# A fixed TensorE order for a state-space stage, and other slabs and banks for the last attentions

## The chip, the cores and the metric

The kernel runs on one core of one Trainium2 chip. The metric is the device time of one launch in microseconds (us); a kernel's time is the median of its runs. Engines are TensorE (PE), VectorE (DVE), ScalarE (ACT), GpSimd (POOL) and SyncE (SP, whose queue issues most DMA transfers).

## What is computed

512 tokens of width 1024 in f32 pass four layers, each with an RMS norm ahead of it and a residual sum behind. The first two are an even layer (sliding-window attention beside a state-space mixer) and an odd one (top-k attention); the others are forgetful (fox) attention and dilated attention, each with a memory attention beside it and a convolutional FFN behind it. What the change touches of the reference:

```
def s5_mixer(u, ...):                       # G=32 groups of 16, P=64 states
    dt = exp(log_dt);  mag = exp(a_re * dt);  ang = a_im * dt
    ab = mag * (cos(ang) + i sin(ang));  bb = ((ab - 1) / a) * b
    bu = einsum('blgh,gph->blgp', ug, bb)
    x  = associative_scan(x[t] = ab * x[t-1] + bu[t])
    y  = einsum('blgp,ghp->blgh', x_re, c_re) - einsum(x_im, c_im) + d_skip * ug
    h  = gelu(y) @ glu_w + glu_b
    return h[..., :W] * sigmoid(h[..., W:])

def even_layer(hn, ...):
    q, k, v, gate_a, u, gate_b = split_cols(hn @ w_in, ...)
    att = swa_sink_attention(rms_norm(q), rms_norm(k), v, sinks, rel_bias) * silu(gate_a)
    ssm = s5_mixer(u, ...) * silu(gate_b)
    return concatenate([att, ssm]) @ w_out

# layers 3 and 4
    mix = fox_attention(q, k, v, log_f)        # or dilated_attention(q, k, v)
    h = h + concatenate([mix, memory_attention(qm, rmsnorm(mem), w_mem_kv)]) @ w_out
    h = h + conv_ffn(rmsnorm(h), ...)
```

## The kernel before

**Products and weights.** Every large product is three PE products of split operands (`mm3`, lines 221 to 223: high by high, low by high, high by low). A weight slab of 256 columns comes by `slab()` (line 196): two pieces, each a raw DMA of 512 KB into one of two raw buffers, a copy on ACT (line 216, the high part `wh`) and a subtraction on DVE or POOL (line 217, the low part `wl`). Slabs live in a ring of two buffers (`wp`), to which a phase may add a third.

**Order.** A scheduler arranges the instructions of each engine by when they can run. Where an order is wanted, code is emitted under `issue_after`; the class `Chain` uses it to line up PE's instructions one by one, and `Steps` puts pieces of work off by so many units. Before the change the attentions use `Chain` and the state-space stage does not.

**State-space stage** (lines 617 to 870). After the `u` products (`u2`), the 32 groups are handled in four quarters. `core_a(qu)` (line 634) makes the matrices of a quarter: `zb` on DVE (lines 650 to 652: two products and a sum, twice), `cp` on POOL (667 to 669), transposes of `zb` on PE (681) that ACT evacuates to `bt`, the product with `cbd` (687), `k0` (697), the turned input `uq` (706) and the product `bu` (715). `core_b(qu)` (line 719) runs the scan in DVE (lines 728 to 745, result `zz`), then the products `yp` on PE (755 on) and a gelu on ACT and DVE. Every second quarter `y` is transposed into `yh` and `yl`. The program's order is a(0), then a(qu+1), b(qu); the query products (eight units of a slab quarter, each with a head norm and a transpose) and the gate products (eight units) stand behind in the program and are moved forward by the scheduler as they fit. Behind the gates `gbr`, a bias row, opens the GLU.

**Attentions 3 and 4** (`attn34`, line 1306). Projections stream 13 slabs, then the units of the attention follow (scores, softmax on ACT, transposes of the probabilities `pt`, values `o`), and each block ends in `finish` (line 906): the output product with four slabs of `w_out`, the residual sum and the next norm, whose scaled block `xn` is transposed by `to_x` (line 272) in two halves, each into a PSUM bank that ACT (`xh`) and DVE (`xl`, line 282) evacuate. All four `w_out` slabs are asked for behind the last projection.

Of the kernel before, what the change touches and what calls it, by code (L numbers as in the profile page):

```python
# [8 lines left out]
F32 = mybir.dt.float32  # L9
# [88 lines left out]
def _build(tc, nc, ctx, t, out, dbg, upto):  # L98
# [97 lines left out]
    def slab(src, r0, kc, pieces, wpool=None):  # L196
# [8 lines left out]
        for k0 in range(0, kc, per):  # L205
            k1 = min(kc, k0 + per)
# [8 lines left out]
            with urgent() if evq[1] else nullcontext():  # L215
                A.activation(hi[:, k0:k1], raw, AF.Copy)  # L216
                eng.tensor_tensor(lo[:, k0:k1], raw, hi[:, k0:k1].bitcast(F32), op=OP.subtract)  # L217
        return hi, lo
# [29 lines left out]
    def norm_scale(hb, gb, xn):  # L248
# [4 lines left out]
        V.tensor_scalar(ss[:, 2:3], ss[:, 0:1], 1.0 / D, EPS, op0=OP.mult, op1=OP.add)  # L253
# [208 lines left out]
    normed = []  # L462

    def norm_half(half):
        for tb in (2 * half, 2 * half + 1):
            normed.append(norm_block1(xin[tb], gb, x1, tb, n0))
# [34 lines left out]
    for i in range(3):  # L501
        PE.transpose(prmps[:, i * 16:(i + 1) * 16], prm[:, i], ident[:16, :16])
# [115 lines left out]
    for cs_ in range(2):  # L618
        w = slab(w_in1, 0, 8, [(1280 + cs_ * 256, 256)])
        for i in range(4):  # L620
            ps = acc()
            tm(ps[:, :256], w, xk(x1, i * 128, i * 128 + 128))
            evac(u2[:, cs_ * 16:(cs_ + 1) * 16, i, :], ps[:, :256].rearrange("p (g x) -> p g x", x=16))
    dump("u2", u2)
# [9 lines left out]
    def core_a(qu):  # L634
# [58 lines left out]
        k0 = sp_.tile([128, 8, 8, 16], F32, tag="k0", name="k0", bufs=2)  # L693
        for th in range(2):
            tp = tps()
            for i in range(4):
                PE.matmul(tp[:, i * 128:(i + 1) * 128], shm[:, th * 4 + i], c7, start=True, stop=True)
            evac(k0[:, :, th * 4:(th + 1) * 4, :].rearrange("p g t o -> p t g o"),
                 tp.rearrange("p (t g o) -> p t g o", t=4, g=8))
# [3 lines left out]
        for g in range(8):  # L703
            for s2 in range(2):
                rs_ = slice(s2 * 64, s2 * 64 + 64)
                PE.matmul(tp[rs_, g * 64:(g + 1) * 64], u2[:, (g % 2) * 16 + g0 + g // 2].rearrange("p i x -> p (i x)"),
                          ident.rearrange("p (c s) -> p s c", s=2)[:, s2], start=True, stop=True)
        A.activation(uq.rearrange("p g c -> p (g c)"), tp, AF.Copy)

        bu = sps()  # L710
        buv = bu.rearrange("p (r g c) -> p r g c", r=2, g=4)
        for i in range(2):
            for g in range(4):
                for q in range(2):
                    PE.matmul(buv[q * 64:(q + 1) * 64, i, g], bt[:, i, g, q * 64:(q + 1) * 64], uq[:, 2 * g + q],
                              start=True, stop=True)
        cst_[qu] = (gs, cp, k0, uq, buv)

    def core_b(qu):
# [10 lines left out]
        zz = sp_.tile([128, 2, 4, 64], F32, tag="zz", name="zz")  # L730
# [6 lines left out]
        for i in range(2):  # L737
# [8 lines left out]
                               op1=OP.subtract)  # L746

        yp = pst("yp")
        ypv = yp.rearrange("p (t g o) -> p g t o", t=8, g=4)
        for g in range(4):  # L750
            for i in range(3):
                for q in range(2):
                    qs = slice(q * 64, q * 64 + 64)
                    if i < 2:
                        PE.matmul(ypv[qs, g], xs[qs, i, g], cp[qs, i, g],
                                  start=i == 0, stop=False)
                    else:
                        PE.matmul(ypv[qs, g], uq[:, 2 * g + q], k0[:, 2 * g + q],
# [952 lines left out]
```

## Time and profile before

| | us |
|---|---|
| three runs, median | 1884.34 (1881.91 to 1887.64) |
| profiled execution | 1881.42 |
| its span | 1879.6 |
| PE busy | 1781.7 (95%) |
| DVE, ACT, POOL busy | 1037.2, 734.8, 150.7 |
| chain that ended last | PE 78%, DVE 10%, DMA 4%, ACT 4%, issue 3% |

The span is what the profiler recorded of one execution; the execution's own time lies 1.8 us above it. The page divides the span into 40 equal slices of 47 us and gives the busy tenths of each engine and the granted PE clock of each, in tenths of full speed. The timeline rows give the idle time of an engine ahead of a group in square brackets, and what ended it. Since PE is busy 95% of the span, what matters is where its waits lie and which clock it was granted.

### The profile page before, as it was taken

The page shows a single profiled execution, that of the slowest core. Times are in us where ns is not written, and L with a number is a line of the kernel's source. Part 1 is how long each engine was busy: PE and PEld are TensorE (multiplying, and loading weights), DVE is VectorE, ACT ScalarE, POOL GpSimd, SP SyncE. Part 2 cuts the span into 40 slices and gives each one's busy share as a digit, 9 for nine tenths or more (in the row PEclk, how much of TensorE's full clock was granted, in tenths as well). Part 3 has the DMA queues.
Part 4 walks back from the last instruction along what each step waited for, and adds up shares of the span by engine and source line. Part 5 has one row for each costly group of instructions (what it writes and reads, how often), then busy time and mean ns, then how long its engine had stood idle before and what let it go on. Part 6 is the DMA issues. An engine that isn't in the chain of part 4 may idle for free.

```text
span 1879.6 us, 27744 instructions
## 1 busy us (share of the span) xinstructions
PE 1781.7 (95%) x11106; PEld 1511.3 (80%) x11108; DVE 1037.2 (55%) x2110; ACT 734.8 (39%) x1460; POOL 150.7 (8%) x159
## 2 busy tenths in 40 slices
PE   6889899999999998989999999999989999999998
PEld 5777689878688886778888888889957888888886
DVE  6865574279855525655655562266276555554522
ACT  5333353353434334543443342233265444333421
POOL 2432101222120000000000000000000000000000
PEclk9899999999999999999999999999999999999999
DMA  5403222312513332003333323333220133332321
GB/s 151 130 13 112 90 90 59 94 57 68 166 42 99 112 112 90 1 1 100 98 105 93 90 68 117 107 124 99 82 90 1 37 113 90 100 102 74 106 90 67
DMA packets 187896, 161.72 MB, mean 86 GB/s; under 512 B 14568, under 2 KB 170320, under 8 KB 187768
## 3 DMA queue, kind: packets, MB, share of 16 engines
q1 hardware_dynamic: 181168, 144.30, 24.8%
q0 software_dynamic: 2784, 9.00, 1.6%
q10 hardware_dynamic: 3816, 6.66, 1.1%
q8 instruction: 87, 1.43, 0.3%
q14 instruction: 41, 0.34, 0.1%
HBM read 157.88 MB, written 4.74 MB: 87 GB/s over the span
## 4 chain that ended last, share of the span: by engine, by line
PE 78%; DVE 10%; DMA 4%; ACT 4%; issue 3%; POOL 1%; SPq 0%; DVEq 0%; ACTq 0%; POOLq 0%
PE acc L221 19%; PE acc L222 19%; PE acc L223 19%; PE misc L351 6%; PE o L351 2%; DVE wl L217 2%; PE tps L351 2%; PE spp L351 1%; ACT wh L216 1%; PE misc L221 1%; PE misc L222 1%; PE misc L223 1%; PE o L1232 1%; ACT p L1475 1%; DMA raw<-in_ev_w_in_dram 1%
## 5 line engine op out<-in xcount | busy, mean ns | idle before, releaser
L217 DVE TENSOR_TENSOR wl<-raw,wh 128x1024 fp32r<-128x1024 f32 (+3 forms) x242 | 296.3, 1234 | 392.3 <-ACT wh L216 392.0
L216 ACT ACTIVATE wh<-raw 128x1024 fp32r<-128x1024 f32 (+2 forms) x262 | 270.2, 1044 | 488.9 <-PE acc L222 208.1
L222 PE MATMUL acc<-xl,wh 128*128 128x512 f32 (+2 forms) x1064 | 402.3, 379 | 0.5 <-DVE xl L282 0.5
L221 PE MATMUL acc<-xh,wh 128*128 128x512 f32 (+2 forms) x1064 | 402.2, 380 | 0.5 <-ACT xh L281 0.5
L223 PE MATMUL acc<-xh,wl 128*128 128x512 f32 (+2 forms) x1064 | 400.7, 377 | 0.0
L223 PEld LDWEIGHTS acc<-xh,wl 128*128 128x128 f32 (+1 forms) x1064 | 201.4, 189 | 39.2
L221 PEld LDWEIGHTS acc<-xh,wh 128*128 128x128 f32 (+1 forms) x1064 | 200.7, 189 | 40.0 <-ACT xh L281 1.0
L222 PEld LDWEIGHTS acc<-xl,wh 128*128 128x128 f32 (+1 forms) x1064 | 201.5, 189 | 39.0 <-DVE xl L282 0.8
L221 PE MATMUL acc<-wh,xh 128*128 128x256 f32 (+1 forms) x704 | 204.6, 291 | 2.4 <-ACT xh L281 1.9
L223 PE MATMUL acc<-wh,xl 128*128 128x256 f32 (+1 forms) x704 | 200.9, 286 | 0.6 <-DVE xl L282 0.6
L222 PE MATMUL acc<-wl,xh 128*128 128x256 f32 (+1 forms) x704 | 200.5, 285 | 0.7 <-DVE wl L217 0.7
L221 PEld LDWEIGHTS acc<-wh,xh 128*128 128x128 f32 x704 | 134.8, 192 | 10.4 <-issue 5.8
L223 PE MATMUL acc<-wh,gl 128*128 128x512 f32 x352 | 139.2, 395 | 0.0
L221 PE MATMUL acc<-wh,gh 128*128 128x512 f32 x352 | 138.5, 394 | 0.0
L222 PE MATMUL acc<-wl,gh 128*128 128x512 f32 x352 | 138.5, 393 | 0.0
L222 PEld LDWEIGHTS acc<-wl,xh 128*128 128x128 f32 x704 | 134.9, 192 | 1.6 <-DVE wl L217 1.0
L223 PEld LDWEIGHTS acc<-wh,xl 128*128 128x128 f32 x704 | 135.0, 192 | 1.2 <-DVE xl L282 1.0
L256 POOL TENSOR_TENSOR rs<-ss,mhalf 128x1 f32<-128x1 f32 x32 | 18.2, 569 | 1413.6 <-DVE ss L254 1341.0
L351 PE MATMUL misc<-wh,ah 128*128 128x256 f32 x280 | 83.9, 300 | 3.8 <-DVE xl L282 3.8
L351 PE MATMUL misc<-wh,al 128*128 128x256 f32 x280 | 81.2, 290 | 2.0 <-DVE al L1514 2.0
L351 PE MATMUL misc<-wl,ah 128*128 128x256 f32 x280 | 81.0, 289 | 0.0
L222 PEld LDWEIGHTS acc<-wl,gh 128*128 128x128 f32 x352 | 66.2, 188 | 15.6
(1380 smaller groups left out, 3057.2 us busy)
## 6 DMA issues: line engine op xcount, KB each, us to landing
raw<-in_w_up_dram SPq DMA_DIRECT2D x176, 256.0 KB, 3.2
raw<-in_w_down_dram SPq DMA_DIRECT2D x44, 512.0 KB, 3.6
raw<-in_od_w_in_dram SPq DMA_DIRECT2D x24, 512.0 KB, 3.5
raw<-in_w_in_dil_dram SPq DMA_DIRECT2D x20, 512.0 KB, 3.5
raw<-in_ev_w_in_dram SPq DMA_DIRECT2D x18, 512.0 KB, 3.7
raw<-in_w_out_dram SPq DMA_DIRECT2D x16, 512.0 KB, 3.9
raw<-in_w_in_fox_dram SPq DMA_DIRECT2D x14, 512.0 KB, 4.6
raw<-in_ev_w_out_dram SPq DMA_DIRECT2D x8, 512.0 KB, 3.4
```

The source lines that it names most:

```text
L216: A.activation(hi[:, k0:k1], raw, AF.Copy)
L217: eng.tensor_tensor(lo[:, k0:k1], raw, hi[:, k0:k1].bitcast(F32), op=OP.subtract)
L221: pe.matmul(ps, lh, rh, start=first, stop=False)
L222: pe.matmul(ps, lh, rl, start=False, stop=False)
L223: pe.matmul(ps, ll, rh, start=False, stop=last)
L256: G.tensor_tensor(r, ss[:, 3:4], mhalf[:, :1], op=OP.pow)
L351: self.last = op(*a, **k).ins
L1232: PE.matmul(pov[:, hd % 4], vt[:, kb, kv * 128:(kv + 1) * 128], pt_[:, kb * 128:(kb + 1) * 128], start=kb == 0, stop=kb == qb)
L1475: A.activation(p2, src, AF.Exp, bias=nm[:, hd:hd + 1], scale=-1.0, accum_out=sm[:, hd:hd + 1])
```

## The change

It has six parts.

1. `slab` can hand back its pieces as closures (`parts`), so that a caller places each piece.
2. At the start a norm block's first sum on DVE is issued behind the block before it, and `keep_warm` adds products of zeros on PE: 20 at the start and 4 behind each of the first two blocks.
3. In the state-space stage one `Chain` orders PE from the `u2` products to the last gate. `core_a` and `core_b` are each split in two: `core_a2` holds `k0` and `bu`, `core_b2` the `yp` products and the gelu; the turn of `y` is put off by `Steps`. The 16 query and gate units become a list from which `fill(n)` takes units between the parts. Slabs are asked for one group ahead.
4. `finish` uses banks `tps` for the second half of a block's transposes (not the last block), and `o` ahead of `misc` in the last block's output product.
5. The memory operands have a pool of their own that ends with the memory projections.
6. Two slabs of `w_out` are loaded during the projections (`wo_early`); the other two go to the ring piece by piece, one each unit from the third.

```diff
-    def norm_scale(hb, gb, xn):
+    def norm_scale(hb, gb, xn, prev=None):
...
-        V.tensor_scalar(ss[:, 2:3], ss[:, 0:1], 1.0 / D, EPS, op0=OP.mult, op1=OP.add)
+        with tc.issue_after(prev) if prev is not None else nullcontext():
+            V.tensor_scalar(ss[:, 2:3], ss[:, 0:1], 1.0 / D, EPS, op0=OP.mult, op1=OP.add)
...
+    def keep_warm(n):
+
+        if not keep:
+            keep["z"] = pp.tile([128, 640], BF, name="zeros")
+            G.memset(keep["z"], 0.0)
+            keep["ps"] = pst("yp")
+        for _ in range(n):
+            PE.matmul(keep["ps"], keep["z"][:, :128], keep["z"][:, 128:], start=True, stop=True)
+    keep_warm(20)
...
-            normed.append(norm_block1(xin[tb], gb, x1, tb, n0))
+            normed.append(norm_block1(xin[tb], gb, x1, tb, n0, normed[-1] if normed else None))
+            if half == 0:
+                with tc.issue_after(turned[0]):
+                    keep_warm(4)
...
-    for cs_ in range(2):
-        w = slab(w_in1, 0, 8, [(1280 + cs_ * 256, 256)])
+    c1 = Chain()
+    groups = [(1280, 4), (1536, 4), (0, 4), (256, 4), (1792, 2), (2048, 2), (768, 2), (1024, 2)]
+    wq = []
+
+    def next_slab():
+        if len(wq) < len(groups):
+            wq.append(slab(w_in1, 0, 8, [(groups[len(wq)][0], 256)]))
...
+    def core_a2(qu):
...
+    def core_b2(qu):
...
+    def y_turn(hf):
...
+    def q_unit(g, i):
+        ps = acc()
+        tm(ps[:, :256], wq[2 + g], xk(x1, i * 128, i * 128 + 128), pe=c1)
+        qn = pj.tile([128, 4, 64], F32, tag="qn", name="qn", bufs=2)
+        head_norm(ps[:, :256], 4, 64, [qn])
+        steps.later(2, lambda: q_turn(qn, g, slice(i, 512, 4)))
...
+    def gate_unit(g, q):
+        ps = acc()
+        fm(ps, wq[4 + g], q * 128, 128, xk(x1), pe=c1)
+        silu2(sp_, (gbt, gat)[g // 2][:, g % 2 * 2 + q], ps)
+
+    fills = [(q_unit, g, i) for g in range(2) for i in range(4)] + [(gate_unit, g, i) for g in range(4) for i in range(2)]
+
+    def fill(n):
+        for _ in range(n):
+            if not fills:
+                return
+            f, g, i = fills.pop(0)
+            if i == 0:
+                next_slab()
+            f(g, i)
+            steps.tick()
...
+    fill(2)
     for qu in range(4):
+        core_a2(qu)
+        core_b(qu)
+        fill(1)
+        if qu > 0:
+            core_b2(qu - 1)
         if qu < 3:
             core_a(qu + 1)
-        core_b(qu)
+        fill(1)
+        if qu == 2:
+            steps.later(1, lambda: y_turn(0))
+        fill(1)
+    core_b2(3)
+    steps.later(2, lambda: y_turn(1))
+    fill(16)
+    steps.drain()
...
-                norm_block(h[:, tb], gb, x, tb, ("misc", "misc"), pl, lambda f: steps.later(4, f))
-
-        tags = ("misc", "o") if last else ("misc", "misc")
+                norm_block(h[:, tb], gb, x, tb, ("misc", "tps"), pl, lambda f: steps.later(4, f))
+
+        tags = ("o", "misc") if last else ("misc", "misc")
...
+        def wo_early():
+
+            if not wop:
+                wop.append(phase(stx, "wo", 2, side="right"))
+            wo.append(slab(w_out_ap, 0, 8, [(len(wo) * 256, 256)], wpool=wop[0]))
...
+                if c > 3:
+                    wo_early()
...
-        wo = wout_slabs(w_out_ap, wpools(stx))
+        ring["extra"] = None
+        ring["lo"] = V
+        wparts = []
+        for c in (2, 3):
+            wo.append(slab(w_out_ap, 0, 8, [(c * 256, 256)], wpool=wp, parts=wparts))
...
+            if i > 1 and wparts:
+                wparts.pop(0)()
```

Three places show what moves. First pair, DVE in the state-space stage, between the scan's table (`et`) and the first quarter's scan; `zb_948` and `zb_1133` are the second quarter's matrix, `zz_1050` and `zz_1079` the first quarter's scan (its rows begin with `ctmp<-sps,et`). Before:

```order
L650 TENSOR_TENSOR ctmp_949<-pb_436,bb_416 128x512
L651 TENSOR_TENSOR ctmp_950<-pb_436,bb_416 128x512
L217 TENSOR_TENSOR wl_1629<-raw_1630,wh_1628 128x1024
L690 TENSOR_TENSOR c7_840<-sps_831,dm_557 128x128
L652 TENSOR_TENSOR zb_948<-ctmp_949,ctmp_950 128x512
L650 TENSOR_TENSOR ctmp_954<-pb_436,bb_416 128x512
L651 TENSOR_TENSOR ctmp_955<-pb_436,bb_416 128x512
L652 TENSOR_TENSOR zb_948<-ctmp_954,ctmp_955 128x512
L728 TENSOR_TENSOR ctmp_1046<-sps_874,et_891 128x512
L729 TENSOR_TENSOR ctmp_1047<-sps_874,et_891 128x512
```

And now, at the end of that scan:

```order
L783 TENSOR_TENSOR ctmp_1087<-zz_1079,et_904 128x512
L442 TENSOR_REDUCE ssh_1122<-sq_1120 128x4
L784 TENSOR_TENSOR ctmp_1088<-zz_1079,et_904 128x512
L249 TENSOR_SCALAR rstd_1124<-ssh_1122 128x4
L786 MEMSET zz_1079 128x8
L787 TENSOR_TENSOR zz_1079<-ctmp_1087,ctmp_1088 128x4x63
L445 TENSOR_TENSOR qn_1119<-acc_1094,rstd2_1126 128x256
L788 SCALAR_TENSOR_TENSOR zz_1079<-ctmp_1087,ctmp_1088 128x4x63
L688 TENSOR_TENSOR ctmp_1134<-pb_467,bb_447 128x512
L689 TENSOR_TENSOR ctmp_1135<-pb_467,bb_447 128x512
L690 TENSOR_TENSOR zb_1133<-ctmp_1134,ctmp_1135 128x512
```

The second quarter's `zb` stood ahead of the first quarter's scan and stands behind it now, with a query norm (`ssh`, `rstd`, `qn`) between.

Second pair, ACT at the start of the fox attention, where `p2` are the first units' exponentials, `pt_` the evacuated transposes of probabilities and `wh` weight copies. Before:

```order
L1475 ACTIVATE p2_7239,sm_7193<-p2_7239,nm_7192 128x512
L1475 ACTIVATE p2_7240,sm_7193<-p2_7240,nm_7192 128x512
L216 ACTIVATE wh_7138<-raw_7140 128x1024
L216 ACTIVATE wh_7138<-raw_7144 128x1024
L1530 ACTIVATE qmT_6109<-misc_7248 128x512
L371 ACTIVATE pt__7293<-tps_7288 128x512
L371 ACTIVATE pt__7300<-tps_7295 128x512
L1475 ACTIVATE p2_7279,sm_7193<-p2_7279,nm_7192 128x512
L1475 ACTIVATE p2_7280,sm_7193<-p2_7280,nm_7192 128x512
L216 ACTIVATE wh_7148<-raw_7150 128x1024
L1475 ACTIVATE p2_7307,sm_7193<-p2_7307,nm_7192 128x512
L216 ACTIVATE wh_7148<-raw_7154 128x1024
```

And now:

```order
L1554 ACTIVATE p2_7254,sm_7208<-p2_7254,nm_7207 128x512
L1554 ACTIVATE p2_7255,sm_7208<-p2_7255,nm_7207 128x512
L216 ACTIVATE wh_7181<-raw_7398 128x1024
L1609 ACTIVATE qmT_6140<-misc_7263 128x512
L216 ACTIVATE wh_7181<-raw_7438 128x1024
L381 ACTIVATE pt__7308<-tps_7303 128x512
L1554 ACTIVATE p2_7294,sm_7208<-p2_7294,nm_7207 128x512
L1554 ACTIVATE p2_7295,sm_7208<-p2_7295,nm_7207 128x512
L381 ACTIVATE pt__7315<-tps_7310 128x512
L1554 ACTIVATE p2_7326,sm_7208<-p2_7326,nm_7207 128x512
L1554 ACTIVATE p2_7327,sm_7208<-p2_7327,nm_7207 128x512
```

Behind the second unit's exponentials two weight copies are left where six stood (the last two of the six come just behind the rows shown).

Third pair, PE at the end of the fox attention, where `o<-pt,vm` are the last values and `xn` the normed blocks. Before:

```order
L278 MATMUL misc_8417<-ident_90,xn_8190 128x128 x4
L351 MATMUL o_8394<-pt__8415,vm_6111 64x128
L278 MATMUL misc_8424<-ident_90,xn_8190 128x128 x4
L1563 MATMUL sps_8633<-ident_90,cr_8628 128x44
L351 MATMUL misc_8478<-wh_7128,ah_8351 128x256
```

And now:

```order
L288 MATMUL misc_8448<-ident_90,xn_8221 128x128 x4
L361 MATMUL o_8425<-pt__8446,vm_6142 64x128
L288 MATMUL tps_8591<-ident_90,xn_8487 128x128 x3
L361 MATMUL o_8509<-wh_7020,ah_8382 128x256
L361 MATMUL o_8509<-wl_7021,ah_8382 128x256
```

The second half of a block no longer goes to `misc`, and the last block's output product begins in `o`.

## Rows read from the trace of the kernel before

**Rows 1.** The page: busy time and share of PE; its clock in 40 slices, in tenths.
```profile
PE 1781.7 (95%) x11106; PEld 1511.3 (80%) x11108; DVE 1037.2 (55%) x2110; ACT 734.8 (39%) x1460; POOL 150.7 (8%) x159
...
PEclk9899999999999999999999999999999999999999
```

**Rows 2.** Windows: stretch, its length; busy us (instructions) by engine, PE clock, DMA share, GB/s.
```profile
84.20:168.90 84.70, 74.74 (x807) 63.91 (x808) 55.41 (x101) 34.43 (x63) 28.42 (x27) 0.94 0.17 57
...
157.40:160.50 3.10, 3.10 (x27) 2.96 (x25) 2.45 (x3) 2.45 (x4) 0.00 (x0) 1.00 0.03 9
...
168.90:210.50 41.60, 41.60 (x182) 33.78 (x181) 16.20 (x12) 10.72 (x15) 12.40 (x7) 1.00 0.39 127
```

**Rows 3.** Timeline of PE: start, length, line, tiles, count [idle before, ended by].
```profile
17.34 0.58 PE L222 MATMUL acc<-xl,wh 128*128 128x256 f32 x1 [0.54 <-DVE xl L282]
...
84.23 3.42 PE L697 MATMUL tps<-c,shm 128*128 128x128 f32 x16 [4.78 <-ACT bt L682]
87.58 1.16 PE L706 MATMUL tps<-ident,u 128*64 128x64 f32 x32
...
89.49 1.15 PE L715 MATMUL sps<-uq,bt 128*64 128x64 f32 x32
```

**Rows 4.** Line 755 (`yp`): busy in a window, as rows 2; what PE waited for (us, times).
```profile
97.00:170.00 73.00, 13.19 (x128) 7.98 (x128) 0.95 0.15 52
...
  DVE zz L744: 6.7, 4
```

**Rows 5.** Timeline of PE at the GLU's start.
```profile
212.05 0.22 PE L878 MATMUL sps<-ident,gbr 8*128 8x8 f32 x1 [1.55 <-DMA gbr<-in_ev_glu_b_dram]
```

**Rows 6.** Timeline of PE at the starts of the fox and the dilated attention.
```profile
740.59 0.47 PE L351 MATMUL o<-pt__7330,vt 128*64 128x128 f32 x1 [4.58 <-DVE pt__7330 L369]
...
1387.84 0.47 PE L351 MATMUL o<-pt__12893,vt 128*64 128x128 f32 x1 [3.40 <-ACT pt__12893 L371]
```

**Rows 7.** Windows at the same two places, columns as in rows 2.
```profile
739.10:745.90 6.80, 5.31 (x30) 3.99 (x30) 6.30 (x14) 4.42 (x8) 0.00 (x0) 0.50 0.49 156
...
1387.60:1391.00 3.40, 3.17 (x20) 2.83 (x21) 2.35 (x5) 1.00 (x4) 0.00 (x0) 0.50 0.71 233
```

**Rows 8.** Timeline of PE at the ends of layer 1's and the fox attention.
```profile
298.46 0.88 PE L278 MATMUL misc<-ident,xn 128*128 128x128 f32 x4 [1.41 <-DVE xl L282]
...
802.11 0.66 PE L278 MATMUL misc<-ident,xn 128*128 128x128 f32 x4 [3.41 <-DVE xl L282]
...
804.18 0.58 PE L351 MATMUL misc<-wh,ah 128*128 128x256 f32 x1 [1.41 <-DVE xl L282]
...
850.80 0.66 PE L278 MATMUL misc<-ident,xn 128*128 128x128 f32 x4 [1.05 <-DVE xl L282]
...
852.86 0.38 PE L351 MATMUL misc<-wh,ah 128*128 128x256 f32 x1 [1.22 <-DVE xl L282]
...
865.52 0.66 PE L278 MATMUL misc<-ident,xn 128*128 128x128 f32 x4 [1.03 <-DVE xl L282]
```

**Rows 9.** Timeline of DVE in the state-space stage.
```profile
83.55 2.85 DVE L652 TENSOR_TENSOR zb<-ctmp 128x512 f32<-128x512 f32 x1
...
90.69 0.69 DVE L728 TENSOR_TENSOR ctmp<-sps,et 128x512 f32<-128x512 f32 x1 [2.24 <-PE sps L715]
...
97.24 0.41 DVE L745 SCALAR_TENSOR_TENSOR zz<-ctmp 128x252 f32<-128x252 f32 x1
...
101.07 0.69 DVE L652 TENSOR_TENSOR zb<-ctmp 128x512 f32<-128x512 f32 x1
```

**Rows 10.** Timelines of ACT and POOL in the state-space stage.
```profile
81.11 1.06 ACT L216 ACTIVATE wh<-raw 128x1024 fp32r<-128x1024 f32 x1 [8.22 <-DMA raw<-in_ev_w_in_dram]
...
83.49 2.35 POOL L217 TENSOR_TENSOR wl<-raw,wh 128x1024 fp32r<-128x1024 f32 x1 [11.12 <-ACT wh L216]
...
102.53 1.29 POOL L667 TENSOR_TENSOR cp<-gt 128x512 f32<-128x512 f32 x1 [6.05 <-PE yp L755]
```

**Rows 11.** The page's DMA issues: tile, queue, count, KB each, median us to landing.
```profile
raw<-in_w_out_dram SPq DMA_DIRECT2D x16, 512.0 KB, 3.9
```

More of the change, by code (lines that the diff above doesn't have):

```diff
@@ L194, in ring_start, with slab @@
         ring["n"], ring["extra"] = 2, extra
-    def slab(src, r0, kc, pieces, wpool=None):
+    def slab(src, r0, kc, pieces, wpool=None, parts=None):
         n = sum(p[1] for p in pieces)
@@ L204, in slab, with part @@
         lo = pl.tile([128, WSZ], F32R, tag="wl", name="wl")[:, :kc * n].rearrange("p (k n) -> p k n", n=n)
-        for k0 in range(0, kc, per):
-            k1 = min(kc, k0 + per)
+        def part(k0, k1):
             raw = rawp.tile([128, 1024], F32, tag="raw", name="raw")[:, :(k1 - k0) * n].rearrange(
@@ L217, in slab @@
                 eng.tensor_tensor(lo[:, k0:k1], raw, hi[:, k0:k1].bitcast(F32), op=OP.subtract)
+        for k0 in range(0, kc, per):
+            f = lambda k0=k0: part(k0, min(kc, k0 + per))
+            if parts is None:
+                f()
+            else:
+                parts.append(f)
         return hi, lo
@@ L500, in _build @@
     prmps = sps()
-    for i in range(3):
-        PE.transpose(prmps[:, i * 16:(i + 1) * 16], prm[:, i], ident[:16, :16])
+    with tc.issue_after(turned[0]):
+        for i in range(3):
+            PE.transpose(prmps[:, i * 16:(i + 1) * 16], prm[:, i], ident[:16, :16])
     pt = pp.tile([128, 3, 16], F32, name="pt")
@@ L692, in core_a @@
                         dm.rearrange("p (q g) o -> p g q o", q=2)[:, gs], op=OP.add)
[L693 to L699, printed above, removed]
         uq = sp_.tile([128, 8, 64], F32, tag="uq", name="uq", bufs=2)
@@ new lines, in _build, with q_turn @@
+    steps = Steps()
+    def q_turn(qn, cs_, sl):
+        tp = pst("ft")
+        for i in range(2):
+            c1.transpose(tp[:, i * 128:(i + 1) * 128], qn[:, 2 * i:2 * i + 2].rearrange("p a d -> p (a d)"), ident)
+        with urgent():
+            A.activation(qT[:, 2 * cs_:2 * cs_ + 2, sl], tp[:, :256].rearrange("p (a t) -> p a t", a=2), AF.Copy,
+                         scale=qgs[:, 0:1])
+    def q_unit(g, i):
[4 more added lines that the diff above has]
+        steps.later(2, lambda: q_turn(qn, g, slice(i, 512, 4)))
@@ new lines, in silu2 @@
+    def silu2(pl, dst, ps):
+        th_ = pl.tile([128, 512], F32, tag="s_", name="s_")
+        with urgent():
+            A.activation(th_, ps, AF.Tanh, scale=0.5)
+            th_, ps = (a.rearrange("p (i j) -> p i j", i=4) for a in (th_, ps))
+            V.scalar_tensor_tensor(by_i(dst), th_, 1.0, ps, op0=OP.add, op1=OP.mult)
+    gbt = ytp.tile([128, 4, 512], F32, name="gbt")
+    gat = l1.tile([128, 4, 512], F32, name="gat")
+    def gate_unit(g, q):
+        ps = acc()
+        fm(ps, wq[4 + g], q * 128, 128, xk(x1), pe=c1)
+        silu2(sp_, (gbt, gat)[g // 2][:, g % 2 * 2 + q], ps)
@@ L1270, in _build, with mem_load @@
         return
-    def mem_load(i, st_):
-        mw = phase(st_, "mw", side="right")
+    def mem_load(i):
+        mx = ExitStack()
+        mw = phase(mx, "mw", side="right")
         gm = mw.tile([128, 1024], F32, name="gm")
@@ L1424, in attn34 @@
             for c in range(3):
+                if c:
+                    wo_early()
                 w = slab(w_in, 0, 8, [(1536 + 256 * c, 256)])
```

116 lines of the change are left out of this document (47 added, 69 removed).

## The prediction

> **What bounds the kernel now.** I read the page first: of a span of 1879.6 us TensorE (PE) is busy 1781.7, so at most some 98 us of idle time plus what the clock costs can be won, and the clock is near full nearly everywhere [rows 1]. The question is therefore which of PE's waits, and which stretches at the lower of its two clock levels (1.2 against 2.4 GHz), the change reaches. Next came the windows by stage: from 84.2 to 168.9 us (the state-space parts, with most of the query products) PE is busy 74.7 of 84.7 us at a granted clock of 0.94; from 168.9 to 210.5 (the gate products) it is busy without a gap [rows 2]. Then the timeline of PE by line, for its waits and their releasers: 4.78 us ahead of `k0` [rows 3], 6.7 in all ahead of the four `yp` products, for core_b's `zz` on VectorE [rows 4], 1.55 at `gbr` [rows 5], 4.58 and 3.40 at the start of the fox and the dilated attention, each with a stretch at clock 0.50 around it or behind [rows 6, 7], and waits of 1 to 3.4 us at the ends of the attentions, where transposes and out-products share the bank `misc` [rows 8]. Last the timelines of VectorE (DVE), ScalarE (ACT) and GpSimd (POOL) in the state-space stage [rows 9, 10].
>
> **The start.** 20 products of zeros, and four behind each of the first two blocks, run while PE would wait; the norm's sums are put in order. The start's two slices of the span already have clocks of 0.9 and 0.8 [rows 1], and the first projection waits only 0.54 us, for DVE's `xl` [rows 3]. That evacuation stands behind two weight subtractions on DVE in the new order as well, and these hang on the transfers of the weights, which nothing makes earlier. The lower bound is the clock's: a tenth of 47 us, of which PE is busy two thirds, gives −3. The upper bound: eight zero products stand ahead of real work, each like a gate product of 41.6 / 182 = 0.23 [rows 2], or 0.46 at the lower level: 3.7 us, say 3. I take 0, as the releaser is a transfer.
>
> **The state-space stage.** The same work is done in both kernels: 74.7 us busy at 0.94 and 41.6 at full clock [rows 2], which at full clock is 70 + 42 = 112 us, over a stretch of 126.3 (84.2 to 210.5). So some 10 us of idle and 4.4 of clock are what the query and gate products between the parts are meant to take. I lay the new order along the clock.
>  - Start of `uq`(0): the second query slab's ACT copy waits 8.22 us for its transfer [rows 10], and stands ahead of the evacuations of `u2` and `bt` in both ACT orders. So PE starts at 84.2 as now: 0.
>  - From there `uq` 1.2 [rows 3], two query units of 3.1 (a window that holds one) [rows 2], `k0` 2 (its 16 products took 3.42 after the wait, at the lower level; I take 2) and `bu` 1.15: `bu`(0) ends near 94.7, where now its reader starts at 90.69.
>  - On DVE core_b's chain of quarter 0 lasts 7.0 us (90.69 to 97.65) [rows 9]. In the new order it stands ahead of the six operations that make the next `zb`, where now these stand ahead of it (the order's first pair). So `zb`(1) is ready at 94.7 + 7.0 + 1 (a query's norm on DVE) + 6 × 0.69 [rows 9] = 106.8, its first half at 104.8. PE has one query unit and a turn to do meanwhile, to 98.1. **A new stall of 6.7.**
>  - Quarter 1 to 2: the cover is a query unit and `yp`, 3.1 + 4.3 = 7.4 (two thirds of each `yp` are line 755, 13.19 / 4 = 3.3 [rows 4]; the rest is half as much at most, I take 1), against DVE's 7.0 + 1 + 1.4 (the gelu's two operations at 0.69) + 2.1 for half of `zb`: 11.5. A stall of 4.
>  - Besides, POOL's `cp` operations, of 1.29 each, wait for a `yp` to give their buffer back (6.05 us in the present order [rows 10]); with `yp` put off by a part they fall beside `zb`(2). One `zb` operation beside POOL's 2.35 us took 2.85 where the others take 0.69 [rows 9, 10]; that is 2.2 lost, and I add 2.5 to this stall. The Trainium skill ("SBUF — State Buffer", section "SBUF: two separate sides") says of this that VectorE and GpSimd share one pair of ports, which one of them holds for a whole instruction while the other stands still; the 2.85 agrees with it, and it speaks against this edit. By a rule of sharing without a lock these 2.5 would be 0.
>  - Quarter 2 to 3: a gate unit (41.6 × 24 / 182 = 5.5 [rows 2]) and `yp` cover 9.8 of some 10: 0. From there on gate units separate everything; the waits of `yp` (6.7 [rows 4]) are gone, and the put-off turns of `y` have their sources ready.
>  - Clock: behind the 4.78 wait the next products ran at the lower level (3.42 for `k0` [rows 3]), and a stall of 6.7 invites the same: 2.5, against 4.4 now.
>
> So 112 + 6.7 + 6.5 + 2.5 = 127.7 against 126.3: +1.4. Behind it, `gbr`'s transfer is issued by ACT behind both evacuations of the last turn and a weight copy, so its wait of 1.55 [rows 5] grows by about two ACT operations and a copy of 1.06 [rows 10]: between 0 and 3, I take +2.6. Together **+4**. The lower end: if `zb`'s operations slip between those of core_b, as POOL's and ACT's waits may allow, both stalls go, −10. The upper: no query norm leaves DVE early and each junction loses another 3 us: +12.
>
> **Attention starts.** The two last weight slabs of w_out are now copied one piece a unit, and the other two during the projections. Now ACT has six weight copies of 1.06 us among the first units' exponentials, after the change two (the order's second pair), and DVE six subtractions less. PE waits 4.58 and 3.40 for a transposed probability that these two engines evacuate [rows 6]. I leave 0.5 of each wait: −4.1 and −2.9. The lower level behind each (5.31 us busy at 0.50, and 3.17 [rows 7]) would take half as long: −2.7 and −1.6. Together **−11.3**; at the ends 0, if the new waits in the units take all of it, and −14. The pieces put among the projections add four copies and four transfers to stretches where PE needs 11 us per slab (two units of the gates' size); a 512 KB transfer lands in 3.9 [rows 11], two per slab 7.8, beside another slab's 7.8: it fits only since the slabs are loaded one ahead (15.6 against two slabs' 22). Costed at nothing; without that cover it is 4.6 us per slab, four times, and I put a few of these into the upper end.
>
> **Tails.** Where two halves of a block's transposes and the next out-product use the bank `misc`, each waits for the evacuation of the one before. With `tps` for the second half and `o` for the last block's first out-product, the second half waits for nothing (the order's third pair).
>  - Fox, 802.1: 3.41 and 1.41 [rows 8]; one evacuation stays to be waited for, the second pair comes off with the 0.66 of the transposes between: −2.1.
>  - The last block of fox: 1.05 + 1.22 + 1.03 [rows 8] = −3.3; in the dilated one the first two recur to 0.01 us, and I take the same −3.3.
>  - Layer 1: 1.41 [rows 8], against one new wait, of the size of the smallest there (1.03), where `misc` is taken again: −0.4, and −1 with what of the lower level goes with it.
>  - Layer 2 has its own order, PE's waits there are not on `misc`: 0.
> Together **−9.7**; bounds −14 and −4.
>
> **The sum.** 0 + 4 − 11.3 − 9.7 = −17 on the profiled execution's 1881.4 us, so 1864.4. That execution lies 2.9 under the median of the three times, 1884.3, within their spread (1881.9 to 1887.6); applied to the median, **1867**.
>
> **Rivals.**
>  - (A) The state-space stage gains: DVE's parts of the quarters interleave better than their order by row suggests, and the units cover what they are meant to. Then the stage is 112 + 2 of stalls: −12 instead of +1.4, and `gbr` as forecast: 1854. For it speaks that 10 us of idle are there [rows 2]; against it that `zb` now stands behind core_b. Chance 0.17.
>  - (B) Slower, by the clock: the two stalls in the state-space stage are followed by the lower level, and since PE then falls behind by as much, each unit's norms and gelus shift, and the level holds. For it: at both attention starts the clock is 0.50 over 3.4 and 6.8 us [rows 7]. The units between are then worth double: of the 112 us about 45 lie between the first stall and the gates. If all 45 run at 1.2 GHz it costs 45, which with −17 is +28: 1912. It ends slower than before from 23 us on (17 plus the 5.7 which a measurement of this kernel can tell from no change, 0.3%): 1890. Against it: behind the 4.78 wait of now, the mean over the whole stretch is still 0.94 [rows 2]. Chance 0.08.
>  - (C) The attention starts give little, because the pieces put off (one per unit, an ACT copy of 1.06 and a subtraction on DVE) come into the evacuation chains of later units, each of which has less slack; the fox window shows DVE busy 6.30 of 6.80 [rows 7]. Then −3 instead of −11.3: 1875, and with the projections' transfers late (two slabs by 4.6) 1884. Chance 0.15.
>  - That the change doesn't do what it says is not open: the order shows each move.
>
> **How the numbers follow.** The forecast has 0.60, (A) 0.17, (B) 0.08, (C) 0.15. The forecast's own range, from the terms' bounds taken half way together, is 1857 to 1877. The range for 8 in 10 reaches from just under (A), 1853, to the near half of (C), 1879; left out are (B), half of (C) and the far side of (A). Faster by over 0.3% means under 1878.7: the forecast but for its end, (A), and about half of (C): 0.81; within it half of (C) and the forecast's end: 0.11; slower 0.08, which is (B).
>
> **What would show it.** State-space: PE's row of the second quarter's `zb` transposes with an idle time of 5 to 7 us released by DVE `zb`; a gap near 4 to 7 at the third; none at the fourth; the last gate product near 212, `gbr` waiting 3 to 4. If the first gap is under 2, (A) holds. Attention: the first `o`<-`pt` row with idle under 1 and no 0.50 window behind; if there are new waits of 1 to 2 us at each of the four next units, (C). Tails: `misc`<-`xn` transposes of the last blocks without wait. The clock of the stretch 84 to 170: 0.95 or more; if it is under 0.8, (B). A wrong sign would come from a mechanism in a stage that I cost at nothing: the start, or transfers in the projections.

## The result, and the profile after

The changed kernel takes 1897.4 us (median of five runs, 1894.2 to 1900.3) against 1884.3: ratio 1.007, 95% interval 1.005 to 1.009. It is slower by 13 us where 17 less were forecast. Its profiled execution took 1900.3 us, with a span of 1898.4; before, 1881.4 and 1879.6.

The page after, the lines that answer to [rows 1]: busy time by engine, and PE's clock in 40 slices of 47 us.

```profile
PE 1795.7 (95%) x11134; PEld 1520.5 (80%) x11136; DVE 1039.6 (55%) x2110; ACT 735.6 (39%) x1460; POOL 154.8 (8%) x160
...
PEclk8878989999999999989999999999999999999999
```

PE is busy 14 us longer. The 28 products of zeros take 10.3 us, so this total says little. But the third and fourth slice (94 to 188 us) have clocks of 0.7 and 0.8 where 0.9 stood. The windows say which stretch. First come two of before, from the end of the wait ahead of `k0` to `gbr` and, longer, from the first `zb` transposes to `gbr`; then the two that answer to them of after, and three stretches in it. The columns are those of [rows 2].

```profile
84.20:212.00 127.80, 116.35 (x988) 97.69 (x988) 72.17 (x113) 46.65 (x80) 40.82 (x33) 0.96 0.24 79
75.20:212.00 136.80, 120.59 (x1026) 101.73 (x1024) 80.03 (x127) 49.55 (x84) 41.52 (x33) 0.96 0.26 86
```

```profile
82.20:236.40 154.20, 129.05 (x1000) 110.38 (x1000) 74.55 (x114) 46.00 (x79) 39.09 (x31) 0.84 0.18 59
72.30:236.40 164.10, 131.80 (x1026) 113.02 (x1024) 82.61 (x129) 48.92 (x83) 39.82 (x31) 0.84 0.21 67
99.50:113.20 13.70, 8.95 (x64) 8.43 (x65) 5.01 (x9) 2.70 (x7) 0.80 (x1) 0.50 0.01 1
133.60:147.30 13.70, 9.32 (x65) 8.79 (x66) 5.54 (x7) 3.33 (x8) 3.97 (x3) 0.50 0.01 1
167.80:181.50 13.70, 9.88 (x61) 8.96 (x62) 5.13 (x6) 2.17 (x4) 3.05 (x2) 0.50 0.00 0
```

The stage takes 26.4 us longer. Of this 13.7 are idle time (154.2 - 129.05 = 25.15 against 127.8 - 116.35 = 11.45) and 12.7 are busy time (129.05 against 116.35) on nearly the same work, 1000 products against 988, at a mean clock of 0.84 against 0.96. The longer windows hold the same 1026 products: 27.3 us more, of which 11.2 are busy time. The three stretches at 1.2 GHz hold 28.2 us of busy time, 14 more than at 2.4 GHz. Each lies on a wait of PE ahead of the next quarter's `zb` transposes; the timeline of PE after (start, length, line, tiles, count, idle before and what ended it):

```profile
82.20 0.59 PE L361 MATMUL tps<-ident,u 128*64 128x64 f32 x6 [7.16 <-ACT bt L720]
...
103.29 1.09 PE L361 MATMUL tps<-ident,zb 128*128 128x128 f32 x4 [6.00 <-DVE zb L690]
105.34 1.09 PE L361 MATMUL tps<-ident,zb 128*128 128x128 f32 x4 [0.96 <-DVE zb L690]
...
135.41 1.08 PE L361 MATMUL tps<-ident,zb 128*128 128x128 f32 x4 [6.48 <-DVE zb L690]
139.07 1.09 PE L361 MATMUL tps<-ident,zb 128*128 128x128 f32 x4 [2.57 <-DVE zb L690]
...
167.00 0.63 PE L361 MATMUL tps<-ident,zb 128*128 128x128 f32 x4 [1.73 <-DVE zb L690]
171.62 1.09 PE L361 MATMUL tps<-ident,zb 128*128 128x128 f32 x4 [4.00 <-DVE zb L690]
...
236.44 0.22 PE L940 MATMUL sps<-ident,gbr 8*128 8x8 f32 x1 [1.48 <-DMA gbr<-in_ev_glu_b_dram]
...
248.70 0.80 PE L361 MATMUL misc<-yh,wh 128*128 128x512 f32 x1 [4.78 <-ACT th__2201 L957]
```

So up to `gbr` the change loses 24.4 us (236.44 against 212.05 [rows 5]); the span ends 18.8 later, so the rest gains 5.6. The rows of the attention starts and of the last blocks, after:

```profile
760.42 0.32 PE L361 MATMUL o<-pt__7315,vt 128*64 128x128 f32 x1 [0.90 <-ACT pt__7315 L381]
...
818.87 0.66 PE L288 MATMUL tps<-ident,xn 128*128 128x128 f32 x4 [1.50 <-ACT pt__7978 L381]
820.77 0.58 PE L361 MATMUL misc<-wh,ah 128*128 128x256 f32 x1 [1.25 <-DVE xl L292]
...
871.89 0.90 PE L288 MATMUL tps<-ident,xn 128*128 128x128 f32 x3 [3.88 <-DVE xn L266]
...
1408.00 0.32 PE L361 MATMUL o<-pt__12905,vt 128*64 128x128 f32 x1 [0.72 <-DVE pt__12905 L379]
```

The starts' waits fell from 4.58 and 3.40 [rows 6] to 0.90 and 0.72, and the place at 802 us [rows 8] from 3.41 + 1.41 to 1.50 + 1.25. Ahead of the last block's output product there is a new wait of 3.88 (and the same 3.88 at 1508.7 in the dilated attention).

### The profile page after: what moved, and what is told of

Read it like the earlier page. It is cut to its first block, busy times and chain, and to the rows that moved or that the text cites. A ratio compares the mean times of both kernels' runs of the same rounds, so it can differ in the third digit from the quotient of the medians.

```text
span 1898.4 us, 27794 instructions
## 1 busy us (share of the span) xinstructions
PE 1795.7 (95%) x11134; PEld 1520.5 (80%) x11136; DVE 1039.6 (55%) x2110; ACT 735.6 (39%) x1460; POOL 154.8 (8%) x160
## 4 chain that ended last, share of the span: by engine, by line
PE 75%; DVE 11%; issue 4%; DMA 4%; ACT 4%; POOL 2%; POOLq 0%; DVEq 0%; ACTq 0%; SPq 0%
PE acc L227 18%; PE acc L229 18%; PE acc L228 18%; PE misc L361 6%; PE acc L361 3%; PE o L361 3%; PE tps L361 2%; DVE wl L217 2%; PE spp L361 1%; DMA gm<-in_norm_mem_dram 1%; PE misc L227 1%; DVE xn L266 1%; ACT wh L216 1%; ACT p L1554 1%; PE misc L228 1%
## 5 line engine op out<-in xcount | busy, mean ns | idle before, releaser
L227 PE MATMUL acc<-xh,wh 128*128 128x512 f32 (+2 forms) x1000 | 375.9, 378 | 3.8 <-ACT xh L291 3.8
L228 PE MATMUL acc<-xl,wh 128*128 128x512 f32 (+2 forms) x1000 | 376.0, 376 | 0.0
L229 PE MATMUL acc<-xh,wl 128*128 128x512 f32 (+2 forms) x1000 | 375.0, 375 | 0.0
L228 PEld LDWEIGHTS acc<-xl,wh 128*128 128x128 f32 (+1 forms) x1000 | 188.4, 188 | 35.9 <-DVE xl L292 0.3
L227 PE MATMUL acc<-wh,xh 128*128 128x256 f32 (+1 forms) x576 | 166.2, 289 | 1.4 <-ACT xh L291 1.4
L229 PE MATMUL acc<-wh,xl 128*128 128x256 f32 (+1 forms) x576 | 163.3, 284 | 1.6 <-DVE xl L292 1.6
L228 PE MATMUL acc<-wl,xh 128*128 128x256 f32 (+1 forms) x576 | 162.9, 283 | 0.0
L227 PEld LDWEIGHTS acc<-wh,xh 128*128 128x128 f32 x576 | 109.5, 190 | 8.7 <-issue 5.8
L229 PEld LDWEIGHTS acc<-wh,xl 128*128 128x128 f32 x576 | 109.6, 190 | 2.1 <-DVE xl L292 2.1
L228 PEld LDWEIGHTS acc<-wl,xh 128*128 128x128 f32 x576 | 109.6, 190 | 0.1
```

The lines of the kernel that those rows point to most:

```text
L227: pe.matmul(ps, lh, rh, start=first, stop=False)
L228: pe.matmul(ps, lh, rl, start=False, stop=False)
L229: pe.matmul(ps, ll, rh, start=False, stop=last)
```

## The experiments

Ratios are against the kernel before, run on the same chip in the same batch, with a 95% interval behind; times are medians. Before took 1884.1, 1885.2 and 1883.0 us in the three batches (e1 to e4, e5 to e8, e9 to e12), so times of different batches compare to about 2 us.

**e1, all but the state-space stage, and e2, that stage alone.** Theory S: the whole loss is made in the state-space stage. Rival R: it takes the other parts beside it. The kernel before got either all parts without this, or this alone:

```diff
     for qu in range(4):
+        core_a2(qu)
+        core_b(qu)
+        fill(1)
+        if qu > 0:
+            core_b2(qu - 1)
         if qu < 3:
             core_a(qu + 1)
-        core_b(qu)
+        fill(1)
```

> The kernel before with every part of the change except the state-space stage (its code, order and fills as before). Theory S (the loss is made in the state-space stage: 24 us later at the bias row than before, while the rest of the change gains): faster than before, about 1871 us (1897 less 26), with PE's stage from the first zb transposes to the bias row back at 137 us. Rival R (the start and the slabs of the last attentions take part in the loss): 1884 or more.

Measured: 1867.1 us, 0.991 (0.989 to 0.993).

> The kernel before with the new state-space stage alone. Theory S: slower than before by about what the stage shows in the trace of after, 24 to 27 us: 1908 to 1911. Rival R (the loss needs the earlier start or the other slabs beside it): under 1895.

Measured: 1912.1 us, 1.015 (1.014 to 1.017), one microsecond above what S expected. The two add up: -17 and +28 against 1884 give +11, and the change has +13. Theory S holds: some 17 us of gain are there, and the state-space stage takes back more. One number was off: in e1 the stretch from the first `zb` transposes to `gbr` took 142.8 us, not 137, with the code of before; it began 2.8 earlier and ended 3.2 later.

**e3, no fixed order.** Theory F: the fixed order makes PE stand still. Rival P: the sequence of the parts does, in whatever PE order.

```diff
-    c1 = Chain()
+    c1 = PE
```

> The changed kernel, but TensorE's order in the state-space stage is left to the scheduler (same code, same sequence of parts and units, no chain). Theory F (the fixed order is what makes PE stand still behind zb: without it other ready products go ahead): the waits of 6.0, 6.5 and 4.0 us ahead of the zb transposes fall under 2 each and the time to 1875 to 1885. Rival P (the sequence of the parts in the program is to blame, since DVE has zb behind the scan either way): waits stay, 1892 or more.

Measured: 1870.8 us, 0.994 (0.992 to 0.995). In PE's timeline of e3 the three places still wait, but less:

```profile
103.77 0.66 PE L719 MATMUL tps<-ident,zb 128*128 128x128 f32 x4 [2.36 <-DVE zb L690]
...
129.38 0.66 PE L719 MATMUL tps<-ident,zb 128*128 128x128 f32 x4 [4.16 <-DVE zb L690]
...
154.73 0.63 PE L719 MATMUL tps<-ident,zb 128*128 128x128 f32 x4 [1.47 <-DVE zb L690]
```

8.0 us in all where the fixed order has 21.7 (6.96 + 9.05 + 5.73). So with the sequence of the change, 27 us hang on the fixed order, and P falls. F's numbers were missed on both sides: the time is 4 us below its range, and two of the waits did not fall under 2, so the sequence has its part too.

**e4, zeros in the waits.** Theory C: half of the loss is the lower clock level behind each wait. Rival W: the waits alone are the loss.

```diff
+        if qu > 0:
+            wps = acc()
+            for _ in range(28):
+                c1.matmul(wps, keep["z"][:, :128], keep["z"][:, 128:], start=True, stop=True)
         bt = sp_.tile([128, 2, 4, 128], F32, tag="bt", name="bt")
```

> The changed kernel with 28 products of zeros (6 us at full clock) ahead of each later quarter's zb transposes, where PE stood still; nothing else. Theory C (half of the stage's loss is the lower clock level that follows each wait): the granted clock from 99 to 181 us stays near 1, the products behind the waits take half as long, the stage is 8 to 14 us shorter: 1884 to 1889. Rival W (the waits alone make the loss, since each quarter hangs on the chain over DVE and not on PE's speed): within 4 us of 1897.

Measured: 1890.0 us, 1.003 (1.002 to 1.004): 7 less than with the change, one microsecond outside what C expected and clearly not W. The stage from `uq`(0) to `gbr` is 5.8 us shorter (148.4 against 154.2), where C had 8 to 14. The windows of e4 on the three stretches of above:

```profile
99.50:113.20 13.70, 12.28 (x87) 9.75 (x86) 5.01 (x9) 2.70 (x7) 0.63 (x1) 0.75 0.01 1
133.60:147.30 13.70, 10.34 (x73) 9.37 (x72) 4.83 (x6) 3.20 (x8) 3.25 (x3) 0.63 0.00 1
167.80:181.50 13.70, 13.70 (x102) 10.63 (x99) 4.88 (x7) 3.33 (x6) 2.67 (x2) 1.00 0.00 1
```

The clock rose from 0.50 to 0.75, 0.63 and 1.00, not to near 1 throughout. In these stretches it stayed low longest where PE still stood still 3.03 us, between the two halves of the third quarter's `zb`. So products that compute nothing save 7 us while `zb` is as late as ever (its first transposes at 103.12 against 103.29): that part of the loss is the clock's. It is a quarter of the stage's 26 us, where C had half; but the lower level went only in part.

**e5, `zb` ahead of the scan.** Theory Z: the waits are six DVE operations that stand behind the scan. Rival D: DVE bounds the quarter in any order, and `yp` waits instead. PE's order stays the fixed one; only the request for `zb` moves.

```diff
-    def core_a(qu):
+    zbs = {}
+
+    def core_z(qu):
...
             V.tensor_tensor(zb[:, i], ta, tb_, op=op)
+        zbs[qu] = zb
+
+    def core_a(qu):
...
     for qu in range(4):
+        if qu < 3:
+            core_z(qu + 1)
         core_a2(qu)
```

> The changed kernel with its fixed TensorE order, but DVE's six operations for the next quarter's zb are asked for ahead of core_a2 and core_b of the quarter in hand, as they stood before the change. Theory Z (PE's waits in the fixed order are those six operations standing behind the scan): the waits ahead of the zb transposes (6.0 + 1.0, 6.5 + 2.6, 1.7 + 4.0) fall under 2 in each quarter, the low stretches behind them go, and the time comes to 1868 to 1876. Rival D (DVE is the chain's bound in whatever order: what zb no longer waits, yp waits): 1888 or more, with waits of like size ahead of yp.

Measured: 1868.1 us, 0.991 (0.989 to 0.992), **29 less than the change**, by the position of six operations per quarter under the fixed order. The window of e5 over the stage, and its timelines of DVE and of PE at the second quarter:

```profile
82.50:209.00 126.50, 118.00 (x1000) 101.04 (x1000) 71.74 (x112) 45.55 (x79) 37.41 (x31) 0.95 0.23 72
```

```profile
86.07 0.69 DVE L692 TENSOR_TENSOR zb<-ctmp 128x512 f32<-128x512 f32 x1
...
94.17 0.69 DVE L779 TENSOR_TENSOR ctmp<-sps,et 128x512 f32<-128x512 f32 x1 [0.59 <-PE sps L361]
```

```profile
97.22 1.03 PE L361 MATMUL tps<-ident,zb 128*128 128x128 f32 x8
...
110.79 0.45 PE L361 MATMUL ft<-ident,qn 128*128 128x128 f32 x1 [3.60 <-DVE qn L445]
```

`zb`(1) is ready at 86.8, in time that DVE had free before the scan began at 94.17, and its transposes wait for nothing. In no quarter do the `zb` transposes or `yp` wait 0.4 us or more, so rival D falls. The stage is 27.7 us shorter (154.2 to 126.5). What is late next is smaller: a query's norm, 3.60 and 1.57.

**e6, the slabs alone; e7, the banks alone; e8, the start alone.** Each term of the sum by itself on the kernel before. Their edits:

```diff
+                if c > 3:
+                    wo_early()
...
-        wo = wout_slabs(w_out_ap, wpools(stx))
...
+        for c in (2, 3):
+            wo.append(slab(w_out_ap, 0, 8, [(c * 256, 256)], wpool=wp, parts=wparts))
...
```

> The kernel before with the slabs of the last attentions alone (two slabs of w_out in the projections, two piece by piece, the memory's own pool). The prediction's term: -11.3, so 1873. Rival (the pieces come into later units): 1880 or more.

```diff
-                norm_block(h[:, tb], gb, x, tb, ("misc", "misc"), pl, lambda f: steps.later(4, f))
-
-        tags = ("misc", "o") if last else ("misc", "misc")
+                norm_block(h[:, tb], gb, x, tb, ("misc", "tps"), pl, lambda f: steps.later(4, f))
+
+        tags = ("o", "misc") if last else ("misc", "misc")
```

> The kernel before with the banks of finish alone. The prediction's term: -9.7, so 1874.5. What the trace of after suggests: a new wait of 3.88 ahead of the second-last block's transposes, in two places, with a low stretch behind, against waits of 3.4 and 3.3 that go: 1881 to 1885.

```diff
+    keep_warm(20)
...
-            normed.append(norm_block1(xin[tb], gb, x1, tb, n0))
+            normed.append(norm_block1(xin[tb], gb, x1, tb, n0, normed[-1] if normed else None))
...
```

> The kernel before with the start alone (ordered norm sums, products of zeros). The prediction's term: 0, so 1884. What the trace of after suggests: the first zb transposes 2 to 3 us earlier, of which the transfer of the second query slab takes back what lies ahead of uq: 1881 to 1884.

Measured: the slabs 1869.2 (0.990, 0.988 to 0.993), the banks 1881.5 (0.999, 0.997 to 1.001), the start 1885.7 (1.000, 0.999 to 1.002). The slabs give 16 by the medians of one batch, 14 to 22 by the interval, where the forecast had 11.3. The spans of the two profiled executions, which are of different batches, differ by 11.4 (1879.6 and 1868.2); a single pair decides less. PE's first values in e6 wait 0.90, as in the change:

```profile
735.03 0.32 PE L357 MATMUL o<-pt__7284,vt 128*64 128x128 f32 x1 [0.90 <-ACT pt__7284 L377]
```

The banks give 3.7 us by the medians, with an interval from 6.4 faster to 1.1 slower; the start gives nothing. So nearly all that e1 gains (1867.1, with slabs, banks and start) is the slabs'.

**e9, the second-last block back in `misc`; e11, the last turn of `y` earlier; e12, both**, all on e5's kernel.

```diff
-                norm_block(h[:, tb], gb, x, tb, ("misc", "tps"), pl, lambda f: steps.later(4, f))
+                norm_block(h[:, tb], gb, x, tb, ("misc", "tps" if tb > 1 else "misc"), pl, lambda f: steps.later(4, f))
...
-    steps.later(2, lambda: y_turn(1))
+    steps.later(1, lambda: y_turn(1))
```

> The kernel of e5 (zb ahead of the scan), and the second-last block of each attention keeps both halves of its transposes in the bank misc. Theory T (with tps free, the transposes of that block were put ahead of the output product and wait 3.88 for their source, in two places, each with 3.4 us at the lower level behind): both waits and stretches go, 1857 to 1862. Rival M (the old waits on misc of 1.0 to 1.2 come back in their place): 1866 to 1869.

> The kernel of e5 with the last turn of y one unit earlier, ahead of the last gate product instead of behind it. Theory J (the wait for gbr and the 1.56 behind it hang on the last turn's evacuations): gbr's wait or the one behind goes, the stage's junction is 1.5 to 3 us shorter, 1865 to 1867. Rival (both hang on the last gate's own evacuation and the release of its buffers): 1868, with the same waits.

> The kernel of e5 with the edits of e9 and e11 together. If the two add up by theories T and J: 1854 to 1860; if neither does anything: 1868 as e5.

Measured: e9 1874.3 (0.995, 0.993 to 0.996), 6 more than e5; e11 1866.4 (0.991, 0.989 to 0.993), 1.7 less by the medians, which the two ratios do not tell apart (e5 has 0.989 to 0.992); e12 1871.2 (0.993, 0.990 to 0.995), between e9 and e5, with single times from 1863.2 to 1873.3. Theory T fell, and so did its rival. The timelines of PE and DVE in e9 say what stands there instead:

```profile
847.14 0.39 PE L361 MATMUL o<-wh,ah 128*128 128x256 f32 x1 [4.48 <-DVE al L1604]
```

```profile
845.08 1.41 DVE L266 SCALAR_TENSOR_TENSOR xn<-h,rs,gb 128x512 f32<-128x512 f32 x2 [0.73 <-POOL rs L264]
846.41 0.68 DVE L1604 TENSOR_TENSOR al<-o,ah 128x512 fp32r<-128x512 f32 x1
```

The transposes no longer wait ahead of the output product, but the product itself waits 4.48 for `al`, the split of the last attended values. DVE does that split behind the whole norm of the second-last block, down to `xn`. The 3.88 of the change was only the first of two waits on the same stretch of DVE. The wait is 0.6 longer than the one that it replaces; where the rest of e9's 6 us comes from is open. In e11 the wait behind `gbr` went from 1.56 to 0.65, and one at the GLU's second product from 4.89 to 2.29: theory J is borne out by the waits, while its gain in time is within the noise.

**e10, e5 without the fixed order.**

```diff
-    c1 = Chain()
+    c1 = PE
```

> The kernel of e5 with TensorE's order in the state-space stage left to the scheduler. Theory Z (late zb under a fixed order was the loss; with zb early the fixed order costs nothing): within 4 us of 1868. Rival F (a fixed order costs by itself, behind the query norms and the turns): 1862 or less. Rival G (the fixed order helps): 1873 or more.

Measured: 1862.1 us, 0.989 (0.987 to 0.990), at F's edge and 2 us under Z's lower end, and the best of all: 21 under the kernel before in its batch. Against e5 it is 6 less by the medians and 4 by the ratios, whose intervals just overlap; the idle time says the same way. Its window over the stage:

```profile
81.90:202.30 120.40, 114.32 (x988) 97.37 (x988) 71.64 (x112) 45.52 (x79) 37.30 (x31) 0.97 0.24 75
```

6.1 us of idle time remain, where e5 has 8.5 and the change 25.2. The four kernels side by side, everything else as in the change:

| median us | `zb` behind the scan | `zb` ahead of it |
|---|---|---|
| fixed TensorE order | 1897.4 (the change) | 1868.1 (e5) |
| scheduler's order | 1870.8 (e3) | 1862.1 (e10) |

The loss needs both: the late `zb` costs 29 us under the fixed order and 9 without it, the fixed order 27 with a late `zb` and 6 with an early one.

## Why the prediction was wrong, step by step

**The sign came out wrong in the state-space stage**, which was put at +4 and is +24.4 at `gbr`. Its steps:
- The work of 112 us at full clock, and the start of `uq`(0): right within 2 us; `uq`(0) waits 7.16 and starts at 82.2, 2 us earlier than taken.
- The first stall, 6.7 by the order of DVE: right, 6.96.
- The second, 4 + 2.5: 9.05. The part put on POOL was short. In the change's timeline of DVE, operations of 0.41 to 0.69 take 0.94 to 1.54 beside the POOL operations that make `cp`:

```profile
129.47 1.17 DVE L788 SCALAR_TENSOR_TENSOR zz<-ctmp 128x252 f32<-128x252 f32 x1
130.67 1.43 DVE L688 TENSOR_TENSOR ctmp<-pb,bb 128x512 f32<-128x512 f32 x1
132.02 1.54 DVE L689 TENSOR_TENSOR ctmp<-pb,bb 128x512 f32<-128x512 f32 x1
...
134.07 1.19 DVE L690 TENSOR_TENSOR zb<-ctmp 128x512 f32<-128x512 f32 x1
135.30 1.43 DVE L688 TENSOR_TENSOR ctmp<-pb,bb 128x512 f32<-128x512 f32 x1
...
137.25 0.94 DVE L689 TENSOR_TENSOR ctmp<-pb,bb 128x512 f32<-128x512 f32 x1
```

  and one of POOL's operations at the same time:

```profile
131.51 1.50 POOL L703 TENSOR_TENSOR gt<-pw,cc 128x512 f32<-128x512 f32 x1
```

  Together some 3.8 us more than alone, against 2.5. What was cited of the Trainium skill ("SBUF — State Buffer", section "SBUF: two separate sides") agrees: DVE's operation of 132.02 ends 0.55 us behind the end of this one of POOL's (133.01), little less than its own 0.69. POOL's took 1.50 where 1.06 stood before, so both sides stood still in turn.
- The third stall, put at 0 since a gate unit and `yp` cover 9.8: 5.73. The cover was right, DVE's side was not: a weight subtraction of 3.33 (beside one of POOL's) stood ahead of the scan, and the gate's own evacuation of 1.05 and `cp` again between `zb`'s operations.
- **Clock, 2.5: the step that failed most.** The sum has 2.5 for the whole stage, against 4.4 before; the busy time of 129.05 on work of 112 puts it at some 17, of which the three stretches hold 14. It was sized for one stall alone, by the wait of 4.78 before, behind which the level was low for 3.4 us; but each of the change's three stalls went with 13.7 us at 0.50, of which PE worked two thirds. A stall of 6 us so cost 6 and 4 to 5 more. e4 shows a part of the clock's share by itself: 7 us back with `zb` still late.

So the waits ahead of `zb` came to 21.7 where 13.2 were forecast, 8.5 more, and the clock to 14.5 more. These two make the 20.4 by which `gbr` came later than forecast, with 2.6 taken off by the rest. Rival (B) named the mechanism, had 0.08, and its range from 1890 to 1912 holds the 1897.4. Its condition, "the level holds", came true only in part: between the three stretches the clock is 1.00. The reason held against it, a mean clock of 0.94 behind the 4.78 wait, was one wait's, and the forecast itself put two more in that place, the first of them longer. Other rows of before were dearer: the wait of 4.58 goes with 6.8 us at 0.50 in which PE was busy 5.31 [rows 7], 2.65 lost, and a wait of 3.73 at 49.7, which the forecast did not look at, goes with 10.5 us at the lower level, in which PE was busy 9.89, 4.9 lost:

```profile
49.50:60.00 10.50, 9.89 (x36) 6.84 (x37) 10.19 (x20) 2.94 (x8) 5.98 (x8) 0.51 0.22 79
```

Two stalls at these prices are 5.3 or 9.8, still too little, but on the right side of 2.5.

**The order that was read was right, and what followed from it was undersized.** That `zb` stands behind the scan was the forecast's first reason, and e5, which undoes that alone, gives 29 us. The first stall's size came out of the same reading, so it was no luck. Rival (A), by which the stage gains, is what e10 does: 202.3 at `gbr` against 212.05.

**Attention starts, -11.3: the mechanism right, the size if anything too small.** 4.58 to 0.90 and 3.40 to 0.72, no 0.50 stretch at either, and 16 us by themselves (e6). Rival (C) fell: the later units have no new waits of 1 to 2 us; two old waits there, of 0.77 and 1.33 in the fox attention, went as well, which the term did not have.

**Tails, -9.7: wrong by 6**, -3.7 by the medians of e7, whose interval (-6.4 to +1.1) excludes the forecast and not 0. The place at 802 gave its 2.1 (4.82 to 2.75). For the last blocks the waits for `misc` (1.05, 1.22, 1.03) were taken as gone, and 3.3 again in the dilated attention, where the third is 0.25. They went, but 3.88 for `xn` stands there now, and a stretch at the lower level with it, where the clock of before was 1.00 (848 to 868 us). The window of after:

```profile
870.90:877.80 6.90, 5.91 (x28) 5.82 (x29) 3.80 (x5) 0.98 (x2) 0.00 (x0) 0.51 0.42 122
```

"The second half waits for nothing" looked at the bank and not at the source. The order's third pair had shown it: its row `tps_8591<-xn_8487` is not the second half of the block in `misc_8448<-xn_8221` but another block, the second-last, whose `xn` is only just being made then. DVE's order moved too. The split `al` of the last values stood ahead of this norm (first row, before; the norm's sums begin at 852.73) and stands behind it (second row, after; `xn` is made from 870.42 on):

```profile
850.66 0.68 DVE L1514 TENSOR_TENSOR al<-o,ah 128x512 fp32r<-128x512 f32 x1
```

```profile
871.75 0.68 DVE L1593 TENSOR_TENSOR al<-o,ah 128x512 fp32r<-128x512 f32 x1
```

So the output product waits for `al` in e9, where the transposes are out of its way. Why the scheduler moved `al` is not shown.

**The start, 0: right in the number (e8), by luck.** The reason was that a transfer holds the start. But the first `zb` transposes do come earlier, 3.1 us in e8 and 2.9 in the change; in e8 the stage behind, unchanged, takes 5.6 us more, and nothing of it reaches the end. **`gbr`, +2.6:** its wait did not grow (1.48). Behind it stand 1.57, and 4.78 at the GLU's second product instead of 1.14; but up to the odd layer's first product of `kiT` 167.7 us pass where 167.0 did, so +0.7.

By parts: e2, e6, e7 and e8 by themselves give +28, -16, -3.7 and +0.6, together +9; the change has +13. In the profiled execution of the change, its slowest, it is +24.4 up to `gbr`, where +4 was forecast, and -5.6 behind it, where -21 was. In e1, with the same code behind `gbr`, the profile has -17.6 there. 7 of these 12 us lie between `gbr` and the odd layer (160.5 us in e1 against 167.7), where the change has the waits of 1.57 and 4.78 and e1 one of 1.29; the rest is open.

## What to carry to other kernels

Before an order is fixed on one engine, read where the operands of each fixed step stand on the other engines: a fixed order can turn a late operand into idle time, and six operations in the wrong place cost 29 us here, 9 with the scheduler's order. Price every new stall with the clock behind it, and look for the dearest row that the trace has for a wait of that size: here 4.78 us of waiting went with 1.5 lost (3.42 for `k0` against 1.95 in the change), and 3.73 us with 4.9. And when a wait for a buffer goes, ask when the data of the next step is ready; the wait may have been its cover.

## What the runs showed that was not expected

- Each of the three stalls of 5.7 to 9 us was followed, and in part covered, by one stretch of the same 13.7 us at 1.2 GHz; before, waits of 3.4 to 4.8 went with 3.4 to 10.5 us.
- Zeros multiplied in the waits, useless otherwise, are worth 7 us (e4).
- A gain of 3 us at the start was lost inside the next stage in two kernels with that stage unchanged: in e1 and e8 the stretch from the first `zb` transposes to `gbr` took 142.8 and 142.5 us, against 136.9, at a mean clock of 0.92 against 0.96. Why the level falls more often there is open.
